# Strassen products of the down projections: one addition to x over two neighbouring PSUM banks

## The chip, the cores and the metric

The kernel runs on one core of one Trainium2 chip. The metric is the time of one execution on the device, in microseconds (us); the median of several runs counts. TensorE (PE) multiplies matrices out of SBUF into PSUM, VectorE (DVE) and ScalarE (ACT) work element by element and read PSUM, GpSimd (POOL) and SyncE (SP) mostly issue transfers. [...]

## What is computed

A trunk of two layers over 512 frames of width 1024. Each layer has a half-step SwiGLU feed-forward network (FFN), a mixer (mLSTM in layer 0, gMLP in layer 1), a second FFN and a gated embedding; after each of these x becomes the layer norm of `alpha * x + sublayer(x)`.

```python
def swiglu_ffn(x, w_gu, w_d):
    g, u = jnp.split(x @ w_gu, 2, axis=-1)
    return (jax.nn.silu(g) * u) @ w_d

def reference(x, p, ln_g, ln_b, ffn1_wgu, ffn1_wd, ...):
    for i in range(DEPTH):
        x = layer_norm(DN_ALPHA * x + 0.5 * swiglu_ffn(x, ffn1_wgu[i], ffn1_wd[i]), ln_g[i, 0], ln_b[i, 0])
        mix = mlstm_mixer(...) if i % N_MIXERS == 0 else gmlp_mixer(...)
        x = layer_norm(DN_ALPHA * x + mix, ln_g[i, 1], ln_b[i, 1])
        x = layer_norm(DN_ALPHA * x + 0.5 * swiglu_ffn(x, ffn2_wgu[i], ffn2_wd[i]), ln_g[i, 2], ln_b[i, 2])
        ple = jax.nn.sigmoid(x @ ple_wg[i] + ple_bg[i]) * (p[i] @ ple_wp[i])
        x = layer_norm(DN_ALPHA * x + ple, ln_g[i, 3], ln_b[i, 3])
    return x
```

SEQ is 512, D_MODEL 1024, the FFN's hidden width 2816, the mixers' inner width 2048. All inputs and the output are float32.

## The kernel before

**Precision.** Every factor is split in two parts, high (rounded to float32r) and low (the rest), and a product is made of three matmuls, high by high, high by low and low by high (`mm3`, lines 279 to 281). ACT makes the high part of a weight (`whi`, line 198), DVE the low part (`wlo`, line 207), or, where a wait is asked for with "dma", ACT and a POOL transfer that accumulates (lines 204 and 205). The two parts of x transposed are `xh` and `xl`.

**x.** The residual stream is one SBUF tile `xt` of [128, 4, 1024]: 128 frames by 4 blocks of frames by the width. Ways down (the last matrix of an FFN or of a mixer) add their result to `xt`; the first addition of a sublayer multiplies `xt` by alpha in the same instruction (line 626), the others are plain additions (line 628).

**Ways down by Strassen.** A way down multiplies the hidden activations by [k, 1024] of weights. Chunks of 512 hidden units (256 in an FFN's first chunk) make a 2 by 2 block product: two halves of the frames, two halves of the inner dimension, two halves of the width. Class `Group` does it with seven products in place of eight. `form` makes the sums of activation blocks in place on DVE and splits them into `fhi` and `flo`; `Weights.forms` does the same for the weights. `product` multiplies: a product covers 256 frames by 512 columns, which are two PSUM banks (e = 0 and 1, 128 frames each), and takes 12 matmuls (6 in an FFN's first chunk). Products 0, 1 and 3 start their banks anew, 2, 4, 5 and 6 add to what is in them: products with an even number use one pair of banks, those with an odd number the other (`self.banks[r % 2]`). After each product `add` adds its two banks to the quarter of `xt` that `TO` names. So product r + 2 writes the banks that the addition of product r reads.

**Order.** The order of every engine's instructions is that of the program (a manual schedule), and waits between engines are placed by the framework from the tiles that instructions read and write. In an FFN's chunk each of the first seven projections up (24 matmuls into a bank "fps") is followed in the program by the addition of the product before (`group.add()`), the activation of the projection, one product (`group.product()`), and the making of a further form (`group.form()`). The projections and the products of the chunk before thus alternate on PE. The mLSTM does the same with a step after each of its projections in a head (`step`, and `group.add()` in `project_v`), with 3 groups, and the gMLP with 2 groups between its gate blocks (`add`, `products`). The four FFNs have 5 groups each; the last chunk of each, and the end of the mixers, go through `down` without Strassen, with banks "dps".

**Banks.** Four banks ("up0" to "up3") rotate among projections; four ("dn0" to "dn3") serve the ways down and some other uses: transposes "xps", gate sums, "vps" of the first head, "nps", "hps", "sps", "gvps", the embedding's "gps". Each `dn_bank` call makes a new tile of one bank with the tag of the bank that was used least recently and is not pinned; a group pins its four banks and gives them back after products 5 and 6.

The addition of a product before is, in `add`, one call of `residual` for each bank:

```python
for e, ps in enumerate(self.banks[r % 2]):
    residual(2 * i + e, j, ps, r in self.first)
    if r >= 5:
        unpin(ps)
```

Of the kernel before, what the change touches and what calls it, by code (L numbers as in the profile page):

```python
# [10 lines left out]
F32 = mybir.dt.float32  # L11
F32R = mybir.dt.float32r
AF = mybir.ActivationFunctionType
OP = mybir.AluOpType
# [3 lines left out]
P = 128  # L18
# [17 lines left out]
ALPHA = (2.0 * DEPTH) ** 0.25  # L36
# [212 lines left out]
def hybrid_trunk(ctx: ExitStack, tc, x, p, ln_g, ln_b, ffn1_wgu, ffn1_wd, ffn2_wgu, ffn2_wd,  # L249
# [21 lines left out]
    ps_dn = ctx.enter_context(tc.tile_pool(name="ps_dn", bufs=1, space=PSUM))  # L271
# [3 lines left out]
    vec, sca, pool = nc.vector, nc.scalar, nc.gpsimd  # L275

    def mm3(ps, st, mv, start, stop, more=False):

        mm(ps, st[0], mv[0], start=start, stop=False, skip_group_check=more)  # L279
        mm(ps, st[0], mv[1], start=False, stop=False, skip_group_check=more)  # L280
        mm(ps, st[1], mv[0], start=False, stop=stop, skip_group_check=more)  # L281
# [9 lines left out]
        return ps_up.tile([P, 512], F32, name=name, tag=f"up{up_order[-1]}")  # L291

    dn_order, pinned = deque(range(4)), {}

    def dn_bank(name, pin=False):

        i = next(i for i in dn_order if i not in pinned.values())
        dn_order.remove(i)
        dn_order.append(i)
        bank = ps_dn.tile([P, 512], F32, name=name, tag=f"dn{i}")  # L300
        if pin:
            pinned[id(bank)] = i
        return bank

    def unpin(bank):
        i = pinned.pop(id(bank))
        dn_order.remove(i)
        dn_order.append(i)

    def tmp_tile(name):  # L310
        return tmp.tile([P, 512], F32, name=name, tag="tmp")
# [158 lines left out]
    xt = act.tile([P, TB, D], F32, name="xt")  # L470
# [19 lines left out]
    def turn_x(t, bank=dn_bank, halves=(0, 1), norm=None):  # L490

        for g in halves:
            ps = bank("xps").rearrange("p (k c) -> p k c", k=4)
            for k in range(4):
                kb = 4 * g + k
                nc.tensor.transpose(ps[:, k], xt[:, t, kb * P:(kb + 1) * P], ident)  # L496
            dst = (slice(None), slice(4 * g, 4 * g + 4), slice(t * P, (t + 1) * P))
            if norm is not None and norm.deferred:
                xf = tmp_tile("xf").rearrange("p (k c) -> p k c", k=4)
                for k in range(4):  # L500
                    sca.activation(xf[:, k], ps[:, k], AF.Identity, scale=col("ln_g", norm.at + 4 * g + k),  # L501
                                   bias=col("ln_b", norm.at + 4 * g + k))
                ps = xf
            sca.activation(xh[dst], ps, AF.Copy)
            vec.tensor_sub(xl[dst], ps, xh[dst].bitcast(F32))
# [6 lines left out]
    def load_columns():  # L512
# [24 lines left out]
        def turn():  # L537
            ps = dn_bank("colps")
            for t, rows in enumerate(tiles):
                m = min(P, NCOL - t * P)  # L540
                nc.tensor.transpose(ps[:, t * P:t * P + m], rows[:m], ident[:m, :m])
            vec.tensor_copy(cols, ps[:, :NCOL])
# [80 lines left out]
    def residual(t, half, ps, first):  # L623
        dst = xt[:, t, half * 512:(half + 1) * 512]
        if first:
            vec.scalar_tensor_tensor(dst, dst, ALPHA, ps, op0=OP.mult, op1=OP.add)
        else:
            vec.tensor_add(dst, dst, ps)  # L628
# [25 lines left out]
    def down(hs, first, norm=None, lazy=False, defer=False):  # L654
# [17 lines left out]

        for t in range(TB):
            banks = [dn_bank("dps"), dn_bank("dps")]
            for k in range(n):
                if k == len(ws):
# [88 lines left out]
    class Group:  # L765
# [36 lines left out]
        def product(self):  # L802
            r = self.next_product
            self.next_product += 1
            w, f = W.take(), self.ready.popleft()
            if r < 2:
                self.banks.append([dn_bank("gps", True) for _ in range(2)])
            for e, ps in enumerate(self.banks[r % 2]):
                for k in range(self.half):
                    i, j = (e, k) if self.by_tokens else (k, e)  # L810
                    mm3(ps, [a[:, i, j * P:(j + 1) * P] for a in f], [a[:, k] for a in w],
                        k == 0 and r in (0, 1, 3), k == self.half - 1, r not in (0, 1, 3))

        def add(self):

            r = self.next_add
            if r == self.next_product:
                return
            self.next_add += 1
            i, j = self.TO[r]  # L820
            for e, ps in enumerate(self.banks[r % 2]):
                residual(2 * i + e, j, ps, r in self.first)
                if r >= 5:
                    unpin(ps)


    def ffn(layer, k, rows, prepare=None):
# [413 lines left out]
    def gmlp():  # L1241
        with stage_pool("extra", EXTRA) as extra, stage_pool("gm_parts") as near, stage_pool("ghpool") as hpool, \
# [112 lines left out]
            def spatial(b, v):  # L1355

                vh, vl = v
                g = b // 2
                bank = dn_bank if b in (1, 3, 15) else up_bank
                banks = [bank("sps").rearrange("p (t e c) -> p t e c", t=2, e=2) for _ in range(2)]  # L1360
                for t in range(TB):
                    ps = banks[t // 2][:, t % 2]
                    mm(ps, vh[:, t], wsp[:, g], start=True, stop=False)
                    mm(ps[:, 1], vl[:, t], wsh[:, g], start=False, stop=True)
                add = mp.tile([P, P], F32, name="gadd", tag="gadd", bufs=2)
                vec.scalar_tensor_tensor(add, rsum[:, g], col("vn_b", b), bsb[:, g], op0=OP.mult, op1=OP.add)
                s = tmp_tile("gs")
                for e, ps in enumerate(banks):
                    dst = s[:, e * 256:(e + 1) * 256].rearrange("p (t c) -> p t c", t=2)
                    vec.scalar_tensor_tensor(dst, ps[:, :, 0], col("vn_g", b), add[:, None, :].to_broadcast([P, 2, P]),  # L1370
                                             op0=OP.mult, op1=OP.add)
                    vec.scalar_tensor_tensor(dst, ps[:, :, 1], col("vn_g", b), dst, op0=OP.mult, op1=OP.add)
                if b + 2 < 16:
                    vs.append(split_v(b + 2))
                return s
# [39 lines left out]
            SPLIT_AT = {10: (8,), 11: (9,), 12: (10, 11), 13: (12, 13), 14: (14,), 15: (15,)}  # L1415
            for b in range(16):
                add()
                if b in (0, 14):
                    ss.extend(spatial(i, vs.popleft()) for i in (b, b + 1))
# [15 lines left out]
                for i in range(n):  # L1435
                    if i:
                        add()
                    products.popleft().product()
                    form()
# [167 lines left out]
```

## Time and profile before

| what | value |
| --- | --- |
| time, median of 3 runs (lowest to highest) | 2227.38 us (2226.92 to 2227.43) |
| span of the profiled execution, first to last instruction | 2225.4 us |
| mean granted TensorE clock | 0.999 |
| bytes moved by DMA | 253.57 MB, mean 114 GB/s |
| MATMUL instructions | 10517 |
| costliest group on ACT: `whi<-wraw`, x340 | 352.2 us |
| costliest group on DVE: `wlo<-wraw`, x292 | 352.7 us |

The page gives the profiled execution's span; its own time around the span is not listed apart, and the median of the runs lies 2.0 us above the span. In a group's row the first number is the busy time in us, the second the mean time of one in ns, and behind the second bar stands the idle time of the engine just before these instructions with what ended it. Two instructions of DVE that follow each other overlap a little, so the busy time of a group can be less than count times mean. In a timeline a row holds the start, the length, the engine, the line and the tiles written and read; "xN" tells how many equal instructions in a row it merges.

### The profile page before, as it was taken

The numbers are of one execution on the slowest core, as the hardware profiler recorded it, in microseconds if no ns is written. First come the engines' busy times: TensorE is split into PE (matmuls) and PEld (weight loads), VectorE is DVE, ScalarE is ACT, GpSimd is POOL, SyncE is SP. The second block draws the span as 40 slices with busy tenths as digits, with TensorE's granted clock in tenths as the row PEclk, the third lists the DMA queues.
The fourth block names the chain that finished last, engine by engine and source line by source line (L and its number), as shares of the span: only waits on it lengthen the run. The fifth ranks groups of instructions, "written<-read, shape, count | busy, mean of one in ns | idle before, by whom it ended". The sixth has DMA issues, their size and how long they took to land.

```text
span 2225.4 us, 26475 instructions
## 1 busy us (share of the span) xinstructions
PE 2214.4 (100%) x10517; PEld 1856.1 (83%) x10517; DVE 1557.3 (70%) x2280; ACT 922.2 (41%) x1308; POOL 104.3 (5%) x135
## 2 busy tenths in 40 slices
PE   9999999999999999999999999999999999999998
PEld 8888888888888888888888888888888888888887
DVE  5666667776776786666687766666788778666677
ACT  4333336464646443333345333335345453333332
POOL 1000000111101100000000000000001100000000
PEclk9999999999999999999999999999999999999999
DMA  7422223466847444332233422223437743332221
GB/s 230 130 95 88 95 86 100 100 143 140 160 117 154 130 133 128 98 106 63 99 123 111 134 92 90 95 85 97 140 76 152 164 129 130 117 114 86 85 86 57
DMA packets 206308, 253.57 MB, mean 114 GB/s; under 512 B 5812, under 2 KB 160564, under 8 KB 206184
## 3 DMA queue, kind: packets, MB, share of 16 engines
q1 hardware_dynamic: 168080, 211.83, 29.4%
q0 software_dynamic: 31488, 25.35, 8.4%
q10 hardware_dynamic: 6616, 14.69, 2.0%
q8 instruction: 83, 1.36, 0.2%
q14 instruction: 41, 0.34, 0.0%
HBM read 224.58 MB, written 2.11 MB: 102 GB/s over the span
## 4 chain that ended last, share of the span: by engine, by line
PE 98%; ACT 1%; DMA 0%; DVE 0%; issue 0%; SPq 0%; DVEq 0%
PE fps L279 13%; PE fps L280 13%; PE fps L281 13%; PE gps L279 8%; PE gps L281 8%; PE gps L280 8%; PE dps L279 2%; PE dps L281 2%; PE dps L280 2%; PE gups L279 1%; PE vps L279 1%; PE zps L279 1%; PE zps L281 1%; PE vps L281 1%; PE gvps L279 1%; PE gups L280 1%
## 5 line engine op out<-in xcount | busy, mean ns | idle before, releaser
L279 PE MATMUL fps<-xh,whi 128*128 128x512 f32 x1312 | 510.7, 389 | 0.0
L280 PE MATMUL fps<-xl,whi 128*128 128x512 f32 x1312 | 510.4, 389 | 0.0
L281 PE MATMUL fps<-xh,wlo 128*128 128x512 f32 x1312 | 510.4, 389 | 0.0
L207 DVE TENSOR_TENSOR wlo<-wraw,whi 128x1024 fp32r<-128x1024 f32 (+1 forms) x292 | 352.7, 1218 | 147.9 <-ACT whi L198 146.8
L198 ACT ACTIVATE whi<-wraw 128x1024 fp32r<-128x1024 f32 (+1 forms) x340 | 352.2, 1048 | 179.0 <-PE fps L280 81.6
L207 DVE TENSOR_TENSOR wlo<-wquarter,whi 128x1024 fp32r<-128x1024 f32 (+1 forms) x140 | 156.5, 1118 | 218.2 <-ACT whi L198 218.2
L281 PEld LDWEIGHTS fps<-xh,wlo 128*128 128x128 f32 x1312 | 246.2, 188 | 51.3
L279 PEld LDWEIGHTS fps<-xh,whi 128*128 128x128 f32 x1312 | 246.3, 188 | 51.2
L280 PEld LDWEIGHTS fps<-xl,whi 128*128 128x128 f32 x1312 | 246.3, 188 | 50.6
L198 ACT ACTIVATE whi<-wquarter 128x1024 fp32r<-128x1024 f32 (+1 forms) x140 | 136.3, 974 | 279.8 <-PE gps L281 209.0
L281 PE MATMUL gps<-whi,flo 128*128 128x512 f32 x644 | 251.1, 390 | 0.0
L279 PE MATMUL gps<-whi,fhi 128*128 128x512 f32 x644 | 251.1, 390 | 0.0
L280 PE MATMUL gps<-wlo,fhi 128*128 128x512 f32 x644 | 251.0, 390 | 0.0
L628 DVE TENSOR_TENSOR xt<-xt,gps 128x512 f32<-128x512 f32 x302 | 193.2, 681 | 0.7 <-PE gps L281 0.7
L856 ACT ACTIVATE sg<-fps 128x512 f32<-128x512 f32 x80 | 47.9, 598 | 228.5 <-PE fps L281 224.3
L281 PEld LDWEIGHTS gps<-whi,flo 128*128 128x128 f32 x644 | 120.9, 188 | 25.7
L280 PEld LDWEIGHTS gps<-wlo,fhi 128*128 128x128 f32 x644 | 120.9, 188 | 25.5
L279 PEld LDWEIGHTS gps<-whi,fhi 128*128 128x128 f32 x644 | 120.9, 188 | 25.5
L284 ACT ACTIVATE fhi<-h 128x512 fp32r<-128x512 f32 (+1 forms) x140 | 80.5, 581 | 142.8 <-DVE h L793 54.4
L285 DVE TENSOR_TENSOR flo<-h,fhi 128x512 fp32r<-128x512 f32 (+1 forms) x140 | 87.2, 635 | 42.9 <-ACT fhi L284 42.9
L598 POOL TENSOR_TENSOR rs<-rs,eps_pow 128x1 f32<-128x1 f32 x32 | 20.6, 643 | 1573.6 <-DVE rs L597 1573.6
L501 ACT ACTIVATE xf<-xps,cols 128x128 f32<-128x128 f32 x160 | 59.8, 454 | 53.5 <-PE xps L496 53.5
(306 smaller groups left out, 3625.8 us busy)
## 6 DMA issues: line engine op xcount, KB each, us to landing
wraw<-in_ffn_wgu_dram SPq DMA_DIRECT2D x79, 1024.0 KB, 6.3
wquarter<-in_ffn_wd_dram SPq DMA_DIRECT2D x64, 512.0 KB, 3.7
wraw<-in_ml_w_in_dram SPq DMA_DIRECT2D x24, 1024.0 KB, 5.5
wlo<-wraw POOLq DMA_DIRECT2D x48, 512.0 KB, 6.6
wraw<-in_gm_w_in_dram SPq DMA_DIRECT2D x15, 1024.0 KB, 5.6
wraw<-in_ffn_wgu_dram SPq DMA_DIRECT2D x17, 512.0 KB, 4.0
wraw<-in_ffn_wd_dram SPq DMA_DIRECT2D x8, 1024.0 KB, 4.9
wraw<-in_ml_w_out_dram SPq DMA_DIRECT2D x8, 1024.0 KB, 5.0
```

The lines of the kernel that those rows point to most:

```text
L198: self.nc.scalar.activation(hi[:, s], src[:, s], AF.Copy)
L207: self.nc.vector.tensor_sub(lo[:, s], src[:, s], hi[:, s].bitcast(F32))
L279: mm(ps, st[0], mv[0], start=start, stop=False, skip_group_check=more)
L280: mm(ps, st[0], mv[1], start=False, stop=False, skip_group_check=more)
L281: mm(ps, st[1], mv[0], start=False, stop=stop, skip_group_check=more)
L284: sca.activation(hi, src, AF.Copy)
L285: vec.tensor_sub(lo, src, hi.bitcast(F32))
L501: sca.activation(xf[:, k], ps[:, k], AF.Identity, scale=col("ln_g", norm.at + 4 * g + k), bias=col("ln_b", norm.at + 4 * g + k))
L598: pool.tensor_tensor(rs[:, 1:2], rs[:, 0:1], eps_pow, op=OP.pow)
L628: vec.tensor_add(dst, dst, ps)
L856: sca.activation(sg, ps, AF.Silu)
```

## The change

The four single-bank tiles become one tile `dn_all` of four banks, made once. `dn_bank` returns one bank of it and no longer pins; `dn_pair` returns two neighbouring banks, 0 and 1 or 2 and 3, where both are free, and pins them; `unpin_pair` gives both back. A group takes pairs, `product` writes one bank of the pair after the other as before, and `add` makes one instruction of [128, 2, 512] that adds both banks to two neighbouring blocks of frames of `xt`, in place of one instruction of [128, 512] for each bank. `down`, the projections and all other users keep their instructions.

```diff
     dn_order, pinned = deque(range(4)), {}
-
-    def dn_bank(name, pin=False):
+    dn_all = ps_dn.tile([P, 4, 512], F32, name="dn_all", tag="dn_all")
+
+    def dn_bank(name):
 
         i = next(i for i in dn_order if i not in pinned.values())
         dn_order.remove(i)
         dn_order.append(i)
-        bank = ps_dn.tile([P, 512], F32, name=name, tag=f"dn{i}")
-        if pin:
-            pinned[id(bank)] = i
-        return bank
-
-    def unpin(bank):
-        i = pinned.pop(id(bank))
-        dn_order.remove(i)
-        dn_order.append(i)
+        return dn_all[:, i]
+
+    def dn_pair(name):
+
+        i = next(i for i in dn_order if not {i, i ^ 1} & set(pinned.values())) & 2
+        for j in (i, i + 1):
+            dn_order.remove(j)
+            dn_order.append(j)
+        pair = dn_all[:, i:i + 2]
+        pinned[id(pair)] = i
+        pinned[id(pair), 1] = i + 1
+        return pair
+
+    def unpin_pair(pair):
+        for key in (id(pair), (id(pair), 1)):
+            i = pinned.pop(key)
+            dn_order.remove(i)
+            dn_order.append(i)
...
             if r < 2:
-                self.banks.append([dn_bank("gps", True) for _ in range(2)])
-            for e, ps in enumerate(self.banks[r % 2]):
+                self.banks.append(dn_pair("gps"))
+            pair = self.banks[r % 2]
+            for e in range(2):
                 for k in range(self.half):
                     i, j = (e, k) if self.by_tokens else (k, e)
-                    mm3(ps, [a[:, i, j * P:(j + 1) * P] for a in f], [a[:, k] for a in w],
+                    mm3(pair[:, e], [a[:, i, j * P:(j + 1) * P] for a in f], [a[:, k] for a in w],
                         k == 0 and r in (0, 1, 3), k == self.half - 1, r not in (0, 1, 3))
...
             i, j = self.TO[r]
-            for e, ps in enumerate(self.banks[r % 2]):
-                residual(2 * i + e, j, ps, r in self.first)
-                if r >= 5:
-                    unpin(ps)
+            pair = self.banks[r % 2]
+            dst = xt[:, 2 * i:2 * i + 2, j * 512:(j + 1) * 512]
+            if r in self.first:
+                vec.scalar_tensor_tensor(dst, dst, ALPHA, pair, op0=OP.mult, op1=OP.add)
+            else:
+                vec.tensor_add(dst, dst, pair)
+            if r >= 5:
+                unpin_pair(pair)
```

## The prediction

> **What bounds the kernel now.** I read three views: the page's head and chain, the stretches, and the waits of TensorE (PE) alone.
>
> ```profile
> span 2225.4 us, 26475 instructions
> PE 2214.4 (100%) x10517; PEld 1856.1 (83%) x10517; DVE 1557.3 (70%) x2280; ACT 922.2 (41%) x1308; POOL 104.3 (5%) x135
> ...
> PE 98%; ACT 1%; DMA 0%; DVE 0%; issue 0%; SPq 0%; DVEq 0%
> ```
>
> PE is busy in 2214.4 of 2225.4 us and is 98% of the chain that ended last. The stretches (length, then PE, PEld, DVE, ACT, POOL) tell where the other 11.0 us lie.
>
> ```profile
> 0.00:21.00 21.00, 18.66 (x137) 17.92 (x138) 8.58 (x15) 8.83 (x14) 8.47 (x19) 1.00 0.99 294
> 21.00:362.00 341.00, 341.00 (x1546) 283.53 (x1545) 222.27 (x283) 124.75 (x165) 1.67 (x3) 1.00 0.33 106
> 362.00:376.00 14.00, 13.95 (x118) 13.75 (x116) 8.41 (x14) 11.11 (x23) 0.55 (x1) 1.00 0.09 20
> 376.00:2216.00 1840.00, 1839.79 (x8717) 1540.09 (x8716) 1312.31 (x1959) 777.12 (x1107) 92.66 (x111) 1.00 0.41 114
> 2216.00:2225.40 9.40, 0.97 (x9) 0.77 (x7) 5.71 (x13) 0.42 (x1) 0.92 (x1) 0.74 0.15 57
> ```
>
> The first 21 us lose 2.3 us (inputs come in) and the last 9.4 us lose 8.4 us (the last normalisation and store); no Strassen product is in either. In the 2195 us between, PE is without work for 0.05 + 0.21 = 0.26 us. TensorE's own waits, all of them:
>
> ```profile
> PE warm L1560 <- POOL ident masks.py:199: 1.4, 1, 1.4
> PE sup L731 <- DVE wlo L207: 0.4, 1, 0.4
> PE sup L731 <- ACT whi L198: 0.3, 1, 0.3
> PE sup L281 <- DVE gbias L557: 0.2, 1, 0.2
> ```
>
> None of them names an addition to xt or a bank "gps". But a busy PE is modelled: a matmul is shown 0.39 us long, so a short hole can hide under the one before. I therefore checked the pitch, in the timeline of one FFN chunk: the first matmul of products 1 to 5 of a group (PE), then the additions of products 0 to 4 (VectorE, DVE; "x2" is the two halves).
>
> ```profile
> 101.54 0.39 PE L279 MATMUL gps<-whi,fhi 128*128 128x512 f32 x1
> 109.70 0.39 PE L279 MATMUL gps<-whi,fhi 128*128 128x512 f32 x1
> 117.86 0.39 PE L279 MATMUL gps<-whi,fhi 128*128 128x512 f32 x1
> 126.02 0.39 PE L279 MATMUL gps<-whi,fhi 128*128 128x512 f32 x1
> 134.18 0.39 PE L279 MATMUL gps<-whi,fhi 128*128 128x512 f32 x1
> ```
>
> ```profile
> 102.45 1.28 DVE L628 TENSOR_TENSOR xt<-xt,gps 128x512 f32<-128x512 f32 x2
> 108.43 1.28 DVE L628 TENSOR_TENSOR xt<-xt,gps 128x512 f32<-128x512 f32 x2
> 118.04 1.28 DVE L628 TENSOR_TENSOR xt<-xt,gps 128x512 f32<-128x512 f32 x2
> 126.20 1.28 DVE L628 TENSOR_TENSOR xt<-xt,gps 128x512 f32<-128x512 f32 x2
> 131.78 1.28 DVE L628 TENSOR_TENSOR xt<-xt,gps 128x512 f32<-128x512 f32 x2
> ```
>
> From product to product lie 12 matmuls of the product and 24 of the projection behind it. The four distances are 8.16 us each, 8.16 / 36 = 0.2267 us a matmul, whatever DVE does meanwhile. The FFN stages run at one fixed pitch with no hole in it.
>
> **The change, part by part.** *Removed and added:* 25 groups (20 in the FFNs, 3 in the mLSTM, 2 in the gMLP) of 7 products make 175 pairs of additions: 350 operations of 128x512 become 175 of 128x1024. By shape, DVE's groups:
>
> ```profile
> L628 DVE TENSOR_TENSOR xt<-xt,gps 128x512 f32<-128x512 f32 x302 | 193.2, 681 | 0.7 <-PE gps L281 0.7
> L793 DVE TENSOR_TENSOR h<-h 128x512 f32<-128x512 f32 x16 | 11.1, 692 | 0.6
> L626 DVE SCALAR_TENSOR_TENSOR xt<-xt,gps 128x512 f32<-128x512 f32 x48 | 30.8, 681 | 0.5 <-PE gps L281 0.5
> L621 DVE TENSOR_TENSOR xt<-xt,gb 128x1024 f32<-128x1024 f32 x20 | 24.5, 1225 | 0.7
> ```
>
> 302 + 48 = 350 agrees. An operation over two banks does not occur before, so I bound it. Lower end: 1225 ns, the SBUF row of 1024 elements, less the 692 - 681 = 11 ns by which a PSUM source is shorter at 512: 1.21 us. Upper end: nothing saved, 2 x 681 = 1.36 us. I take 1.22 us, beside the row of the same size. The pair does not cost 1.36 us today: two in a row overlap and take 1.28 us. So a pair saves 0.06 us (at most 0.07, at worst it costs 0.08), and DVE is lighter by 175 x 0.06 = 10.5 us of 1557.3 (between 12 lighter and 14 heavier). All of it lies beside PE, which is busy throughout and waits for no addition: 0 us on the path.
>
> [...]
>
> *The start of an addition moves:* it needs both banks, so it waits for the product's last matmul, where the first half could start 6 matmuls earlier. Who waited for a bank "gps":
>
> ```profile
> DVE xt L628: 0.7, 2
> DVE xt L626: 0.5, 1
> ```
>
> Three additions of 350 ever waited for PE. At the other 172 pairs DVE comes late (above: product 1 begins at 101.54, and the addition of product 0, long complete, only at 102.45). There the wait adds nothing. One of the three, in the mLSTM, and what DVE does next:
>
> ```profile
> 544.68 0.68 DVE L626 SCALAR_TENSOR_TENSOR xt<-xt,gps 128x512 f32<-128x512 f32 x1
> 545.89 0.69 DVE L626 SCALAR_TENSOR_TENSOR xt<-xt,gps 128x512 f32<-128x512 f32 x1 [0.53 <-PE gps L281]
> 546.49 2.48 DVE L1161 TENSOR_TENSOR hf<-hps,sz 128x512 f32<-128x512 f32 x4
> ...
> 551.84 1.23 DVE L207 TENSOR_TENSOR wlo<-wraw,whi 128x1024 fp32r<-128x1024 f32 x1 [1.67 <-ACT whi L198]
> ```
>
> The single operation would start at 545.89 and let DVE go at about 547.03 (1.22 less the overlap of 0.08) in place of 546.49: 0.54 us late. Behind it stand the four multiplications into hf and the two splits, for which only ACT waits; ACT's whi is then the next link, and DVE's 1.67 us of idle time before 551.84 is the cover. Without that cover it is 0.5 us a place, 1.6 us for three.
>
> *The banks come free later:* both at the end of the pair, not one halfway. Product r+2 writes the banks that product r's addition reads. In the FFN rows that is 109.70 + 8.16 - 109.71 = 8.2 us of room after the addition of product 1 (108.43 + 1.28). The tightest place that I found in the whole trace is product 2 in the mLSTM:
>
> ```profile
> 578.51 1.28 DVE L628 TENSOR_TENSOR xt<-xt,gps 128x512 f32<-128x512 f32 x2
> ```
>
> ```profile
> 580.31 0.39 PE L279 MATMUL gps<-whi,fhi 128*128 128x512 f32 x1
> ```
>
> 580.31 - 579.79 = 0.52 us, and 0.58 with an operation of 1.22. At the upper end of 1.36, 0.44 is left. It occurs once in each of three heads.
>
> *The rotation of banks:* a pair must now be banks 0-1 or 2-3. A group always pins all four, and all other uses between groups come in twos (the transposes, "nps", "hps", "dps") apart from the start and the gates; the least recently used pair stays the one that came free first. By following the list of free banks through the stages I find no user that gets a bank sooner after its last reader than before. 0 us. DMAs and their queues are not touched.
>
> **Sum:** 2225.4 + 0 = 2225.4 us of span, with the 2.0 us by which the median lies above this execution's span (2227.38 - 2225.4): **2227.4 us**. About 0.2% (4.5 us) is what a measurement of this kernel can tell from no change.
>
> **Rivals.** *A, a wait for the whole tile (slower).* The four banks are now one tile. If the first matmul of a product had to wait until every earlier addition out of that tile was over, and not those of its own banks, product r+1 would wait for addition r. From the rows: addition 0 ends at 103.73 against 101.54 (2.19 late), 1 at 109.71 against 109.70 (0.01), 2 at 119.32 against 117.86 (1.46), 3 at 127.48 against 126.02 (1.46), 4 at 133.06 against 134.18 (in time). That is 5.1 us a group, 25 x 5.1 = 128 us: 2355 us. It decides from the first product on, as margins are spent already. For it: no tile before spans several banks. Against it: xt is one tile as well, PE transposes a part of it while DVE adds to others, and the list of PE's waits has no xt. 5%.
>
> *B, the coarser operation is late on the path.* If the late start is not covered at the three places, and the end of the pair hits PE: +1.6 us, 2229.0; with the upper bound's 14 us on DVE a little of that again. [...] 6%.
>
> *C, PE has room that a lighter DVE uncovers (faster).* In the mLSTM, matmuls are slower than in the FFNs (min/median/max, in ns, of a stretch in the mLSTM, then of one in an FFN, and the matmuls of the whole mLSTM):
>
> ```profile
> L280 PE MATMUL gps<-wlo,fhi x19: 392/396/396, 564.7 to 599.1; 128*128 128x512 f32 x19
> ```
>
> ```profile
> L280 PE MATMUL gps<-wlo,fhi x26: 389/389/389, 1222.3 to 1288.3; 128*128 128x512 f32 x26
> ```
>
> ```profile
> 376.00:768.00 392.00, 392.00 (x1935) 1.00 0.60 138
> ```
>
> 396 ns against 389, 7 ns. The 0.26 us without work, and 7 ns on as many as 1935 matmuls of the stretch from 376 to 768 us, are 13.8 us: 2213.6 if DVE were the cause and went away. But it gives back 21 x 0.06 = 1.3 us there. 3%, two of them over 0.2%.
>
> [...]
>
> *D, the change is not what it says* (the operation is cut at the bank border again): 350 operations, 2227.4. 2%.
>
> **How the numbers follow.** Forecast 84%, A 5, B 6, C 3, D 2. Slower by over 0.2%: A and 1 of B, 6%. Faster: 2 of C, 2%. Within 0.2%: 92%. The range, 2225.0 to 2230.5, holds the forecast, D and B with its 1.6 us and as much again for the upper bound of the operation, and downward C's smaller part; A is left out.
>
> **What would show it.** DVE's instructions fall by 175 to 2105, its busy time to about 1547 us; the 128x1024 form xt<-xt,gps appears 175 times at about 1.22 us; PE keeps 8.16 us from product to product and its list of waits has no gps or xt. I am wrong if PE's busy time or its pitch moves, if a wait of PE for xt appears (A: after every product), or if the new operation takes over 1.36 us.

## The result, and the profile after

The changed kernel takes 2606.43 us (median of 4 runs, 2605.39 to 2607.91) against 2227.27 us before: 1.1704 times as long, 95% interval 1.1687 to 1.172. No change was forecast. The page's head and its chain of work:

```profile
span 2606.2 us, 26336 instructions
PE 2326.2 (89%) x10517; PEld 1895.5 (73%) x10517; DVE 1552.5 (60%) x2105; ACT 926.8 (36%) x1308; POOL 103.7 (4%) x135
...
PE 68%; DVE 20%; ACT 8%; issue 4%; DMA 1%; ACTq 0%; POOL 0%; DVEq 0%; POOLq 0%
```

TensorE has the same 10517 matmuls, but 280.0 us of the span without work (2606.2 - 2326.2) where there were 11.0, and VectorE, which had no share in the chain, now holds 20% of it. TensorE's own waits, the longest of the list (waiting line, releaser, us in total, times, longest):

```profile
PE dn_all L279 <- DVE xt L837: 91.0, 61, 2.5
PE dn_all L279 <- DVE xt L638: 46.8, 22, 3.7
PE dn_all L279 <- DVE pad L1013: 22.9, 3, 7.6
PE dn_all L279 <- DVE xt L835: 22.2, 9, 4.8
PE dn_all L279 <- DVE pg L1546: 13.5, 14, 2.4
PE dn_all L506 <- DVE xl L515: 10.4, 7, 1.8
PE dn_all L506 <- DVE xt L638: 10.0, 3, 3.8
PE dn_all L279 <- DVE gvf L1329: 9.5, 11, 1.6
```

Every row is a matmul into `dn_all` that waits for a reader of `dn_all`. Lines 835 and 837 are the new additions of the groups; line 638 is the addition behind `down`, whose code did not change; `pg`, `xl` and `gvf` are the readers of single banks in the embedding, the transposes and the gated MLP. (The memset `pad` stands right behind the addition of product 0 in the mLSTM; the list names it in that addition's place.) The same FFN chunk as before in the timeline: the first matmuls of products 0, 1, 3 and 4, and the additions of products 0, 2 and 3:

```profile
103.79 0.39 PE L279 MATMUL dn_all<-whi,fhi 128*128 128x512 f32 x1
114.22 0.47 PE L279 MATMUL dn_all<-whi,fhi 128*128 128x512 f32 x1 [2.10 <-DVE xt L837]
...
133.90 0.47 PE L279 MATMUL dn_all<-whi,fhi 128*128 128x512 f32 x1 [1.38 <-DVE xt L837]
143.68 0.47 PE L279 MATMUL dn_all<-whi,fhi 128*128 128x512 f32 x1 [1.38 <-DVE xt L837]
```

```profile
112.85 1.21 DVE L837 TENSOR_TENSOR xt<-xt,dn_all 128x1024 f32<-128x1024 f32 x1
...
132.54 1.21 DVE L837 TENSOR_TENSOR xt<-xt,dn_all 128x1024 f32<-128x1024 f32 x1
142.32 1.21 DVE L837 TENSOR_TENSOR xt<-xt,dn_all 128x1024 f32<-128x1024 f32 x1
```

Product 1 writes the second pair of banks. The addition of product 0 reads the first pair and ends at 112.85 + 1.21 = 114.06; product 1 begins at 114.22. Products 3 and 4 do the same, 0.15 us behind the end of the addition before. So the wait is not for the banks that are written, but for the tile. The whole trace agrees: none of the 436 reads of `dn_all` by VectorE and ScalarE overlaps a matmul into `dn_all`. The distance from product 0 to 1 is 10.43 us in place of 8.16, and from 3 to 4 it is 9.78.

A second loss hides in TensorE's busy time, which grew by 111.8 us (2326.2 - 2214.4). Behind the hole at 114.22 (timeline), and the clock in the stretch around it (length, busy, matmuls, granted clock, transfers):

```profile
115.94 0.63 PE L279 MATMUL dn_all<-whi,fhi 128*128 128x512 f32 x1
116.37 0.63 PE L280 MATMUL dn_all<-wlo,fhi 128*128 128x512 f32 x1
116.80 0.63 PE L281 MATMUL dn_all<-whi,flo 128*128 128x512 f32 x1
```

```profile
113.00:120.00 7.00, 5.79 (x18) 0.76 0.34 109
```

The matmuls stand 0.43 us apart, not 0.227, and the granted clock is 0.76 in these 7 us. I took the distances between the starts of neighbouring matmuls from the traces and sorted what exceeds the pitch of the shape: as a hole where it is over 0.23 us, else as slower pitch. The clock records of the same traces give the time at half clock; the last stretch of each row lies behind the last matmul.

```
kernel                               span    holes   slower   half clock: stretches, us
before                              2225.4     1.4     12.2      1     6.8
after                               2606.2   304.4     89.9     41   168.4
one tile, single additions          2617.8   309.8     96.1     45   184.9
two lasting tiles of two banks      2320.4    73.9     34.7     12    57.6
fresh tiles of two banks            2248.4    19.1     17.4      3    13.0
fresh tiles, more places            2227.1     2.5     12.7      1     5.6
change, holes filled                2578.7   227.9     59.4     20    97.3
```

From before to after that is 303.0 us of holes and 77.7 us of slower pitch, 380.7 of the 380.8 us. Of the holes 145 us lie ahead of products of the groups, 57 ahead of blocks of `down`, and 102 ahead of the other users of the four banks (the transposes, the gated MLP and the embedding above all).

### The profile page after: what moved, and what is told of

Read it like the earlier page. It is cut to its first block, busy times and chain, and to the rows that moved or that the text cites. A ratio compares the mean times of both kernels' runs of the same rounds, so it can differ in the third digit from the quotient of the medians.

```text
span 2606.2 us, 26336 instructions
## 1 busy us (share of the span) xinstructions
PE 2326.2 (89%) x10517; PEld 1895.5 (73%) x10517; DVE 1552.5 (60%) x2105; ACT 926.8 (36%) x1308; POOL 103.7 (4%) x135
## 4 chain that ended last, share of the span: by engine, by line
PE 68%; DVE 20%; ACT 8%; issue 4%; DMA 1%; ACTq 0%; POOL 0%; DVEq 0%; POOLq 0%
PE dn_all L279 11%; PE dn_all L281 10%; PE dn_all L280 10%; PE fps L279 7%; PE fps L280 7%; PE fps L281 7%; DVE wlo L207 5%; ACT whi L198 4%; DVE xt L837 3%; DVE flo L285 2%; ACT fhi L284 2%; ACT xf L511 1%; DVE xt L638 1%; PE sup L741 1%; PE zps L279 1%
## 5 line engine op out<-in xcount | busy, mean ns | idle before, releaser
L279 PE MATMUL dn_all<-whi,fhi 128*128 128x512 f32 x660 | 272.1, 412 | 131.6 <-DVE xt L837 85.0
L281 PE MATMUL dn_all<-whi,flo 128*128 128x512 f32 x660 | 265.2, 402 | 0.0
L279 PEld LDWEIGHTS dn_all<-whi,fhi 128*128 128x128 f32 x660 | 127.5, 193 | 189.2 <-issue 125.6
L280 PE MATMUL dn_all<-wlo,fhi 128*128 128x512 f32 x660 | 264.8, 401 | 0.0
L837 DVE TENSOR_TENSOR xt<-xt,dn_all 128x1024 f32<-128x1024 f32 x151 | 183.2, 1213 | 3.4 <-PE dn_all L281 3.3
L279 PE MATMUL dn_all<-whi,xh 128*128 128x512 f32 (+1 forms) x304 | 125.4, 413 | 49.1 <-DVE pg L1546 13.5
L281 PEld LDWEIGHTS dn_all<-whi,flo 128*128 128x128 f32 x660 | 128.1, 194 | 28.8
L280 PEld LDWEIGHTS dn_all<-wlo,fhi 128*128 128x128 f32 x660 | 128.1, 194 | 24.9
L280 PE MATMUL dn_all<-wlo,xh 128*128 128x512 f32 (+1 forms) x304 | 120.6, 397 | 0.0
L281 PE MATMUL dn_all<-whi,xl 128*128 128x512 f32 (+1 forms) x304 | 120.2, 395 | 0.0
```

The costliest lines, as they stand in the source:

```text
L837: vec.tensor_add(dst, dst, pair)
```

## The experiments

The theory: a matmul into a PSUM tile waits until every earlier read out of that tile is over, whichever of its banks was read; with one tile of four banks this holds up everything that had four tiles. Rival 1: the two-bank addition itself is waited for, as it starts late and frees both banks late. Rival 2: the rotation by neighbouring pairs makes users meet on the same bank.

### One tile, single additions

```diff
-            dst = xt[:, 2 * i:2 * i + 2, j * 512:(j + 1) * 512]
-            if r in self.first:
-                vec.scalar_tensor_tensor(dst, dst, ALPHA, pair, op0=OP.mult, op1=OP.add)
-            else:
-                vec.tensor_add(dst, dst, pair)
+            for e in range(2):
+                residual(2 * i + e, j, pair[:, e], r in self.first)
```

> Keeps the one tile of four banks and the pairing of banks, but adds each bank with an operation of its own, as before. Theory (any matmul into the tile waits for all earlier reads out of it, whichever bank they read): 2590 to 2620 us, the same waits of TensorE for additions to xt, granted clock near 0.97. Rival 1 (the two-bank addition itself is what is waited for, since it starts late and frees both banks late): back near 2227 us. Rival 2 (the new rotation of banks by neighbouring pairs makes users collide on the same bank): as in the theory, about 2600; the next two kernels tell these two apart.

Measured: 2616.42 us, ratio 1.1749 (1.1725 to 1.1772), clock 0.965. TensorE's waits begin:

```profile
PE dn_all L279 <- DVE xt L638: 141.8, 84, 3.7
PE dn_all L279 <- DVE pad L1010: 23.1, 3, 7.7
PE dn_all L279 <- DVE xt L636: 22.4, 9, 4.9
```

With the change's operation taken out its loss stays whole: rival 1 falls. The kernel is even some 10 us longer than with the pair operation; between the two profiled executions in the table 5.4 us of that are holes and 6.2 us slower pitch. Two operations of together 1.28 us that end later than one of 1.21, now that the end is on the path, would fit the holes; this was not tested apart.

### Two lasting tiles of two banks

```diff
-    dn_all = ps_dn.tile([P, 4, 512], F32, name="dn_all", tag="dn_all")
+    dn_two = [ps_dn.tile([P, 2, 512], F32, name=f"dn_two{i}", tag=f"dn_two{i}") for i in range(2)]
...
-        return dn_all[:, i]
+        return dn_two[i // 2][:, i % 2]
...
-        pair = dn_all[:, i:i + 2]
+        pair = dn_two[i // 2][:, 0:2]
```

> The change with two lasting tiles of two banks in place of one of four; the rotation of banks and the two-bank addition stay. Theory: a product no longer waits for the addition before it, and the ways down without Strassen are free as well (their 145 us and 54 us of holes go); what is left is waits between two neighbours in one tile (transposes, the embedding's and the gated MLP's banks: some 95 us of holes in the changed kernel, about half of them left, with their share of the slower clock), so 2250 to 2330 us. Rivals 1 and 2: 2580 to 2620 us, since operation and rotation are those of the change.

Measured: 2321.38 us, ratio 1.0424 (1.0403 to 1.0445). The operation and the rotation are those of the change, so rival 2 can hold at most the 94 us that are left. Four of the waits:

```profile
PE dn_two L506 <- DVE xl L515: 13.4, 6, 3.8
PE dn_two L279 <- DVE xl L515: 10.6, 4, 3.9
PE dn_two L279 <- DVE pg L1546: 8.8, 7, 2.4
PE dn_two L279 <- DVE gvf L1329: 6.4, 6, 1.6
```

No addition to `xt` is in the list. What still waits I read as neighbours in one tile; the view does not name the banks. In the FFN chunk products 0, 1 and 2 are at the old distance, and product 1 begins ahead of the addition of product 0:

```profile
100.87 0.39 PE L279 MATMUL dn_two<-whi,fhi 128*128 128x512 f32 x1
...
109.03 0.39 PE L279 MATMUL dn_two<-whi,fhi 128*128 128x512 f32 x1
...
117.19 0.39 PE L279 MATMUL dn_two<-whi,fhi 128*128 128x512 f32 x1
```

```profile
109.94 1.21 DVE L837 TENSOR_TENSOR xt<-xt,dn_two 128x1024 f32<-128x1024 f32 x1
```

109.03 - 100.87 = 117.19 - 109.03 = 8.16 us. Over the trace 157 of the 436 reads of `dn_two` have a matmul into `dn_two` that starts while they run, where with one tile there was none.

### Fresh tiles of two banks, with the pair operation and without

```diff
+    def dn_pair(name, pin=False):
 
         i = next(i for i in dn_order if i not in pinned.values())
...
+        pair = ps_dn.tile([P, 2, 512], F32, name=name, tag=f"dn{i}")
...
+    def dn_bank(name):
+        return dn_pair(name)[:, 0]
...
-            banks = [dn_bank("dps"), dn_bank("dps")]
+            banks = dn_halves("dps")
```

Here i is one of two pairs; users of two banks at once ("dps", "nps", "sps") take the halves of one tile. The second kernel differs by the single additions of the first experiment.

> The change as it was priced: the two-bank addition, on a tile of two banks that is made anew at each use; a user of one bank takes such a tile alone, so single users rotate over two places and not four. Theory: no wait of TensorE for an addition, 2222 to 2235 us, clock 0.999, and VectorE at about 1547 us. Rival 1: 2580 to 2620 us, as the operation is unchanged. Rival 2: well over 2235 us, since single users now have still fewer places.

> As the kernel with tiles of two banks made anew, but each bank is added by an operation of its own. Theory: the same time as that kernel within 0.2%, with VectorE's busy time about 10 us longer (1557 us): the two-bank operation is worth nothing on the path. Rival 1: 2227 us here against about 2600 there.

Measured: 2251.46 us (ratio 1.0109, 1.0094 to 1.0124) with the pair operation, 2251.49 us (1.0107, 1.009 to 1.0124) with single additions. On the path the operation is worth nothing; VectorE's busy time is 1546.9 us with it and 1557.7 us without. But the 24 us above the kernel before lie outside the theory's 2222 to 2235 us, and on the side that rival 2 had named for this layout. The waits of the first of the two kernels, without those at the program's start:

```profile
PE gvps L279 <- DVE gvf L1328: 4.8, 2, 3.5
PE xps L506 <- DVE pg L1545: 3.6, 2, 2.3
PE xps L506 <- DVE xt L638: 3.0, 2, 1.5
PE xps L506 <- DVE xl L515: 2.1, 3, 1.0
PE gps L279 <- DVE pg L1545: 1.8, 2, 1.0
...
PE xps L506 <- DVE gvf L1328: 0.8, 1, 0.8
```

The groups are free; what waits are users of one bank, which here have two places in place of four. So a rotation with few places does cost something; but with 24 us for two places, little of the change's 379 us can be put down to its rotation over four.

### The same with more places

```diff
-            return lambda: turn_x(t, halves=(half,), norm=norm)
+            return lambda: turn_x(t, up_bank if (t, half) == (TB - 2, 1) else dn_bank, (half,), norm)
...
-                    ps = dn_bank("gvps")
+                    ps = (up_bank if t % 2 else dn_bank)("gvps")
...
-                        ps = dn_bank("gps")[:, :m]
+                        ps = (up_bank if e % 2 else dn_bank)("gps")[:, :m]
...
-    turn_x(1)
+    turn_x(1, up_bank)
```

> As the kernel with tiles of two banks made anew (2251.5 us), but users of one bank take turns with a bank of the projections' four: every second bank of the gated MLP's first stage and of the embedding, one of the four transposes at a stage's start, and the second block at the program's start. Theory (the 24 us left there are 12 holes at users of one bank that had two places in place of four, and two stretches of half clock after the longest): most of them go, 2226 to 2236 us. If something else in the two-bank tile costs the 24 us (the products or the additions): 2248 to 2254 us. Faster than 2222 us: no theory expects it.

Measured: 2228.86 us, ratio 1.0008 (0.9999 to 1.0017): no difference from the kernel before that this measurement can tell. TensorE's waits are down to the start and to fractions of a microsecond, and the new operation stands in VectorE's groups by shape:

```profile
PE warm L1574 <- POOL ident masks.py:199: 1.4, 1, 1.4
PE sup L281 <- DVE gbias L567: 0.4, 1, 0.4
PE xps L506 <- ACT xf L511: 0.3, 1, 0.3
```

```profile
L837 DVE TENSOR_TENSOR xt<-xt,gps 128x1024 f32<-128x1024 f32 x151 | 183.3, 1214 | 2.4 <-PE gps L281 2.3
L835 DVE SCALAR_TENSOR_TENSOR xt<-xt,gps 128x1024 f32<-128x1024 f32 x24 | 29.2, 1215 | 1.2 <-PE gps L281 1.1
```

These are the change's 175 pair additions, of 1.21 us, with tiles that keep the pairs apart and some users of one bank moved to the projections' banks: the end is where it was.

### Holes filled with useless work

```diff
             w, f = W.take(), self.ready.popleft()
+            if r in self.filled:
+                warm(10)
...
+            if t:
+                warm(10)
             banks = [dn_bank("dps"), dn_bank("dps")]
```

`warm` multiplies the identity into a bank of the projections; the same stands before the blocks of the gated MLP and the embedding.

> The change, with ten useless transposes of 128x128 (about 1.1 us) in front of 73 places where TensorE was found waiting (product 1 of the FFNs' groups and product 3 of their first, every block but the first of the ways down without Strassen, of the gated MLP's first stage and of the embedding); 80 us of work is added, and no wait is taken away. Theory (the 168 us at half clock come from holes of 2.3 us and more, and holes of 1.5 us are followed by none): the fillers lie in the holes, the long holes become short, and some 25 of the 41 stretches of half clock go, at about 1.9 us each: 2545 to 2580 us, clock near 0.985. Rival (the slower clock has another cause, or the fillers only delay): 2606 us or more, up to 2686, clock 0.968.

Measured: 2580.47 us, ratio 1.1587 (1.1571 to 1.1603): 26 us less than the change, with 730 more matmuls, and 0.5 us above the upper end of what was expected. Product 1 of the chunk shown above, and TensorE's line of the page:

```profile
112.72 1.25 PE L1585 MATMUL warm<-ident 128*128 128x128 f32 x10
114.98 0.47 PE L279 MATMUL dn_all<-whi,fhi 128*128 128x512 f32 x1 [1.01 <-DVE xt L842]
115.29 0.40 PE L280 MATMUL dn_all<-wlo,fhi 128*128 128x512 f32 x1
115.52 0.40 PE L281 MATMUL dn_all<-whi,flo 128*128 128x512 f32 x1
115.76 0.40 PE L279 MATMUL dn_all<-whi,fhi 128*128 128x512 f32 x1
```

```profile
PE 2366.8 (92%) x11247; PEld 1953.9 (76%) x11247; DVE 1552.2 (60%) x2105; ACT 926.9 (36%) x1308; POOL 103.8 (4%) x135
```

The fillers take up a part of the hole, the wait that is left is 1.01 us, and the matmuls behind it keep close to the full pitch (0.23 and 0.24 us apart from 115.29 on, not 0.43). By the table 20 of the 41 stretches at half clock are left (I had thought 16) and the slower pitch falls by 30.5 us. That the slower clock follows from the long holes is thus shown; from which of them it did, the last section reads from the clock records.

## Why the prediction was wrong

**The bound, the pitch and the cover were right.** TensorE was the bound at a pitch without holes, and with tiles that keep pairs apart the result is 1.0008 times the time before.

**The operation was priced right.** 1.22 us was taken and 1.21 measured, 2105 instructions were expected and counted, and where nothing else disturbs it VectorE is busy for 1546.1 us in the last layout with pairs (about 1547 was forecast). The late start at three places and the later freeing of banks cost nothing visible there either.

**The step that failed is the term of 0 us for the banks, and with it rival A's 5%.** The sum set the banks' cost to 0 by following which bank is written and which is read. The program did not wait by bank inside the one PSUM tile (none of the 436 reads overlaps a matmul into it): in place of the 0 us stand 303 us of holes and 77.7 us of slower pitch. I had written against A that `xt` is one tile as well and that TensorE transposes a part of it while VectorE adds to others. That observation is right (in the trace before 49 of the 256 transposes begin while VectorE writes to `xt`), but `xt` is an SBUF tile that TensorE reads, and `dn_all` a PSUM tile of several banks that it writes; the trace before had none of these. Which of the two differences decides, no run shows. The one doubt named for A, that no tile before spans several banks, was worth more than 5%.

**A's size was short, above all by two terms that were left out.** Its price was 5.1 us a group and 128 us in all; the holes ahead of the groups' products are 145 us. The sixteen groups of full FFN chunks have 5.35 us each, close to the price, with the 2.19 and 1.46 us worked out from the rows before coming back as 2.10 and 1.38 us in the timeline, beside the short part that a modelled matmul hides; the three groups of the mLSTM have 8.5 us each. Not priced were the other users of the tile, 57 us at `down` and 102 us at the rest, though each of them has a margin of the same kind to be checked. Nor was it priced that TensorE was granted half its clock behind long holes (41 stretches in all, 168.4 us): 77.7 us.

**B, C and D** did not come about: the pair operation alone changes nothing in either direction, a VectorE that is 10 us lighter uncovers nothing, and the operation was not cut.

## What to carry to other kernels

Merging buffers into one tile so that an operation could span them also merged their dependences here (with one tile none of the 436 reads ran beside a matmul into it): before pricing the operation, ask for every writer of the merged tile which readers it may now wait for, and take the margins of all users from the trace. Evidence on how waits are placed for one kind of tile need not carry over to another; here a tile for each pair that is used together kept the wide operation and its dependences apart. And a hole in a TensorE that was full can cost more than its length: the 303 us of holes here brought 77.7 us of slower pitch with them.

## What the hardware showed that was not expected

Behind some holes of 2.3 us beyond the pitch, far apart, TensorE was granted half its clock for 3.4 us: behind the one that the timeline of the changed kernel shows at 114.22 (2.10 us idle), the granted clock was 0.50 from 115.36 to 118.77 us and 1.00 from there on. Of the sixteen holes of that length in the FFNs' chunks four were followed by such a stretch, of the 32 holes of 1.5 us none.

The four differ from the other twelve in where they lie in time. In this trace the 41 stretches begin at multiples of 3.41333 us from each other, to within 0.002 us (the first at 9.545 and the last at 2600.261 us lie 759 times that length apart). If the trace is cut at these times into parts of that length, each of the four holes lies whole in one part, while a border cuts each of the other twelve, so that no part holds more than 1.74 us of it. Of all parts between the first matmul and the last that began at full clock, the 34 with more than 2.06 us of holes were each followed by a stretch, of the 669 with less than 1.95 us none was, and of the ten between six were. So in this execution it went with the time at which a hole came whether it cost its own length alone or a stretch at half clock as well; what sets these times, no run shows.
